# Low parts of weights for the second mixer, made in the first feed-forward, kept in DRAM and read back a pair of tiles ahead

## The chip, the cores and the metric

The kernel runs on one core of a Trainium2 chip (trn2). The metric is the device time of one execution in microseconds; the median of three executions of the kernel before is 2540.43 us (2537.12 to 2541.62). TensorE is PE in the profile, its weight load PEld, VectorE DVE, ScalarE ACT, GpSimd POOL and SyncE SP. All DMAs of the kernel before are issued by SP.

## The reference

Two blocks follow each other. The first has two layers over 256 tokens of a latent and 256 of a context, 1024 wide. A layer is a mixer and a feed-forward, each modulated from a condition vector (adaLN) and closed by a gated residual and a layer norm. In the second layer the context is needed only for keys, values and states, so that layer works on 256 columns where the first works on 512. The second block, two layers of another kind, follows and is not touched. What the change concerns is the mixer of the second layer of the first block:

```python
def _latent_mixer(h, mem, cos, sin, p):
    proj = h @ p['w_in']
    k, v, kg, vg, gf, gb = _mem_parts(proj[..., :MEM_COLS], p)
    q, qg, r, glu, gates = _rest_parts(proj[..., MEM_COLS:], p)
    ...
    o_att = _attend_blocks(_apply_rope(q, cos, sin), k_all, v_all)
    o_gla, _, _ = _gla_bidir(qg, kg, vg, gf, gb, s_f, s_b)
    return _merge(o_att, o_gla, r, glu, gates, p)

def _conv_module(glu, p):
    a, g = jnp.split(glu, 2, axis=-1)
    y = a * jax.nn.sigmoid(g)
    pad = CONV_WIDTH // 2
    y = lax.conv_general_dilated(y, p['conv_w_dw'].astype(y.dtype), (1,), [(pad, pad)], ...)
    y = jax.nn.silu(_layernorm(y, p['conv_ln_g'], p['conv_ln_b']))
    return y @ p['w_conv_o']

def _merge(o_att, o_gla, r, glu, gates, p):
    ...
    g_att, g_gla, g_conv = jnp.split(jax.nn.sigmoid(gates), N_BRANCH, axis=-1)
    return (g_att * y_att + g_gla * y_gla + g_conv * y_conv) @ p['w_out']
```

The conv is depthwise, 31 taps wide over 1024 channels, and its layer norm goes over the channels. All is in float32.

## The kernel before

A float32 product is made of three matmuls of reduced-width operands. Each weight tile is split into a high part `whi` (a cast by ACT) and a low part `wlo` (raw minus high, a subtraction by DVE, on some tiles by POOL); each activation is kept as `hi` and `lo`. `mm_fm` and `mm_tm` then add high x high, high x low and low x high into one PSUM tile (L386 to L388 and L467 to L469). Weights are loaded as 1 MB `raw` tiles by SP, two buffers (`rp`); `whi` and `wlo` have three buffers each (`hp`, `lp`). One `raw` of 256 columns by 1024 rows gives two tiles of 128 columns in `fm`; in `proj_tm` it holds four row tiles of 512 columns, split two at a time. `wsplit` makes the parts of both.

The program is traced by Python and ordered by a list scheduler: every engine runs its instructions in the order that it gives, and `pri` moves an instruction forward or back in priority. Work beside the projections is put into lanes (`bg`): a lane is a list of generators and a rate, and each tile of a projection calls `tick`, which advances every lane by its rate in steps. A lane is emptied by `flush`.

The mixer of a layer (`mixer`) projects the conv's columns a and g first, in four pairs of tiles; after each pair (`L1504`) a generator `conv` is put into the lane "conv" with the rate CRATE0 in the first layer and CRATE1 in the second. It does two channel tiles: one ACT instruction and then 30 taps for each tile, `ca<-gt,cw,ca` on DVE, two taps per tile in a step; at the end POOL adds the two tiles into `cs`. Then come the projections of k and v (512 columns), of q (2 x 512), the columns for the gated linear attention (GLA, with its decay logs, `gla_logs`, on ACT), and of the GLA's values. Merge 0 multiplies the attention's output by `w_att_o` and by its gate; the gate tiles are ACT's `mt`. After it the lanes "gla" and "conv" are emptied, and `conv_norm` begins: a matmul of `cs` with `ones_d` (L1347) gives the mean of all channels, and then come subtraction, squares, their sum, the scale, tanh and the split into `hi` and `lo`. Merge 2 is that of the conv: eight gate tiles are projected ahead (PRE2), beside `conv_norm` and the GLA's scores, and then the conv's output, which needs `conv_norm`'s end.

The first feed-forward is that of layer 0, over 512 columns. Beside it the lane "ada" makes the second layer's modulation. Both are emptied before the second closing norm of that layer.

Places in the profile: the first feed-forward runs from about 825 to 1225 us, the second mixer from 1225 to about 1720. In the latter a, g and k lie in 1226 to 1300, q in 1300 to 1350, GLA's logs in 1400 to 1475, merge 0 to about 1503, merge 2 from there.

```python
    self.bg("conv", [self.conv(l, (m, m + 1), glu, acc, csum, cw, len(xs))], (CRATE0, CRATE1)[l])
    ...
    merge(0, "w_att_o", oatt, PRE0[l], ("heads", "att"), None if GLE[l] else logs)
    self.flush("gla", "conv")
    self.bg("conv", [self.conv_norm(l, acc, csum, ocv, T)], (NRATE0, NRATE1)[l])
    merge(2, "w_conv_o", ocv, PRE2[l], ("conv",))
```

Of the kernel before, what the change touches and what calls it, by code (L numbers as in the profile page):

```python
# [9 lines left out]
F32 = mybir.dt.float32  # L10
# [15 lines left out]
CRATE1 = 1.0  # L26
# [4 lines left out]
CP = 600  # L31
PLO0A = 0
# [155 lines left out]
class Builder:  # L188
    NU = 71

    def __init__(self, ctx, tc, ins, out, dbg=None, stop=None):
# [20 lines left out]
        self.lp = P(name="lp", bufs=3)  # L212
        self.pm = P(name="pm", bufs=3, space=PSUM)
# [143 lines left out]
    def wsplit(self, src, shape, pri=None):  # L357
        hi = self.hp.tile(list(shape), F32R, tag="whi", name=self.nm("whi"))
        lo = self.lp.tile(list(shape), F32R, tag="wlo", name=self.nm("wlo"))
        self.nsplit += 1  # L360
        with self.pri(self.wpri if pri is None else pri):
            self.nc.scalar.copy(hi, src)  # L362
            on_pool = self.pool_lo and self.nsplit % self.pool_lo == 0
            after = self.lo_behind.pop() if self.lo_behind else None
            with self.tc.issue_after(after.ins) if after else nullcontext():
                self.tt(lo, src, hi.bitcast(F32), ALU.subtract, self.nc.gpsimd if on_pool else None)
        return hi, lo

    def fm(self, w, c0, ncols, nk=8):

        raw = None
        for m in range(ncols // 128):
            if m % 2 == 0:
                raw = self.load_raw(w, 0, nk, c0 + m * 128, min(256, ncols - m * 128))
            o = (m % 2) * 128
            yield self.wsplit(raw[:, :, o : o + 128], (128, nk, 128))

    def mm_fm(self, out, W, a, nk=8, first=True, last=True):
# [5 lines left out]
        for k in range(nk):  # L384
            mm = self.nc.tensor.matmul
            mm(out, lhsT=hi[:, k, :], rhs=a.hi[k], start=(first and k == 0), stop=False)  # L386
            mm(out, lhsT=hi[:, k, :], rhs=a.lo[k], start=False, stop=False)  # L387
            mm(out, lhsT=lo[:, k, :], rhs=a.hi[k], start=False, stop=(last and k == nk - 1))  # L388
# [82 lines left out]
    def proj_tm(self, specs, nk, a, tts, consumer, hold=0, mid=None, between=None, ks=None, late=None, held=None, need=None, hook=False):  # L471
# [8 lines left out]
        for part, kl in enumerate((ks[: nk - hold], ks[nk - hold :])):  # L480
# [8 lines left out]
            for h, (w, r0, c0, ncols) in enumerate(specs):  # L489
                for run in runs:  # L490
# [6 lines left out]
                    for k2 in range(0, n4, 2):  # L497
# [3 lines left out]
                        hi, lo = self.wsplit(raw[:, k2 : k2 + n2, :], (128, n2, ncols))  # L501
                        for t in tts:
                            for k in range(n2):
                                kk = run[k2 + k]
                                self.mm_tm(ps[t, h], a, t, kk, (hi[:, k, :], lo[:, k, :]), kk == ks[0], kk == ks[-1])
# [1254 lines left out]
    def layer1(self, l):  # L1760
# [33 lines left out]
        if l == 0:  # L1794
            self.bg("ada", [self.ada(1, (1, 0, 4, 3, 2, 5))], AD1)
        if T == 512:
# [10 lines left out]
            self.flush("ada")  # L1807
# [373 lines left out]
```

## Time and profile before

| what | value |
|---|---|
| median of three executions | 2540.43 us (2537.12 to 2541.62) |
| profiled execution, its own time | 2540.03 us |
| its span | 2538.2 us, mean granted clock 0.982 |
| PE, DVE, ACT, POOL busy | 2405.4, 1624.2, 1180.4, 521.2 us |
| DMA | 345.39 MB, mean 136 GB/s; HBM written 1.05 MB |
| DMA queues | SP's q1 41.5% of the 16 engines' span, instruction queues 0.4% |

The profile is one execution. The page gives busy time by engine; the table by windows gives the same for any stretch; the waits name, for each line of an engine, what it stood for; the timeline lists single instructions with the idle time before them in brackets and what ended it. A busy share over the whole span says little: stretches with different limits lie behind each other.

### The profile page before, as it was taken

How to read it: one execution, taken by the hardware profiler on the slowest of the kernel's cores; microseconds unless marked ns; L12 is line 12 of the kernel's file. 1: busy time of each engine (PE TensorE's matmuls, PEld its weight loads, DVE VectorE, ACT ScalarE, POOL GpSimd, SP SyncE). 2: the span in 40 equal slices, each digit the busy share in tenths (PEclk: the TensorE clock that was granted, in tenths of full speed). 3: DMA queues.
4: the chain of work that ended last, by engine and by line, in shares of the span. 5: the costliest groups of instructions: out<-in, count | busy, mean ns of one | idle time of the engine just before them, and what ended most of it. 6: DMA issues, size and time to landing. Idle time of an engine off the chain costs nothing. (4 is left out here: it accounts for less than half of the span.)

```text
span 2538.2 us, 38571 instructions
## 1 busy us (share of the span) xinstructions
PE 2405.4 (95%) x15163; PEld 2066.3 (81%) x15163; DVE 1624.2 (64%) x2700; ACT 1180.4 (47%) x2225; POOL 521.2 (21%) x460
## 2 busy tenths in 40 slices
PE   7989999899999999999889987998999999999998
PEld 4767887688877777778879887888987899887997
DVE  5878997984365433343899597676625656556564
ACT  3223577654343322232536945654443644446443
POOL 1002003790014000003310006531072100102001
PEclk9999999999999999999999998999999999999999
DMA  8432212223433545553342252643664246543454
GB/s 256 150 136 73 84 31 90 67 84 117 133 102 131 183 150 183 166 183 100 92 129 92 68 166 84 196 137 96 211 208 149 85 150 219 198 144 106 153 192 149
DMA packets 277689, 345.39 MB, mean 136 GB/s; under 512 B 12894, under 2 KB 208888, under 8 KB 277508
## 3 DMA queue, kind: packets, MB, share of 16 engines
q1 hardware_dynamic: 277508, 342.94, 41.5%
q8 instruction: 119, 1.95, 0.3%
q14 instruction: 62, 0.51, 0.1%
HBM read 341.85 MB, written 1.05 MB: 135 GB/s over the span
## 5 line engine op out<-in xcount | busy, mean ns | idle before, releaser
L386 PE MATMUL pm<-hi,whi 128*128 128x256 f32 (+1 forms) x2824 | 917.8, 327 | 24.5 <-ACT mt L298 13.1
L388 PE MATMUL pm<-hi,wlo 128*128 128x256 f32 (+1 forms) x2824 | 909.6, 323 | 6.8 <-DVE wlo L288 6.6
L387 PE MATMUL pm<-lo,whi 128*128 128x256 f32 (+1 forms) x2824 | 910.7, 323 | 4.1 <-POOL lo L288 2.7
L362 ACT CAST whi<-raw 128x1024 fp32r<-128x1024 f32 (+1 forms) x464 | 484.5, 1049 | 829.4 <-PE pm L387 518.9
L288 DVE TENSOR_TENSOR wlo<-raw,whi 128x1024 fp32r<-128x1024 f32 (+2 forms) x437 | 550.9, 1264 | 423.5 <-ACT whi L362 400.0
L386 PEld LDWEIGHTS pm<-hi,whi 128*128 128x128 f32 x2824 | 540.2, 192 | 69.8 <-ACT mt L298 13.9
L388 PEld LDWEIGHTS pm<-hi,wlo 128*128 128x128 f32 x2824 | 541.1, 192 | 52.4 <-DVE wlo L288 8.9
L387 PEld LDWEIGHTS pm<-lo,whi 128*128 128x128 f32 x2824 | 542.0, 192 | 48.3 <-issue 4.1
L291 DVE SCALAR_TENSOR_TENSOR ca<-gt,cw,ca 128x242 f32<-128x242 f32 (+28 forms) x480 | 267.4, 608 | 0.2
L467 PE MATMUL pm<-whi,hi 128*128 128x512 f32 x536 | 212.8, 397 | 7.9 <-DVE qn L288 3.6
L468 PE MATMUL pm<-wlo,hi 128*128 128x512 f32 x536 | 210.6, 393 | 8.9 <-DVE wlo L288 7.7
L469 PE MATMUL pm<-whi,lo 128*128 128x512 f32 x536 | 210.2, 392 | 0.0
L288 POOL TENSOR_TENSOR s<-s,mhalf 128x1 f32<-128x1 f32 (+2 forms) x82 | 66.9, 816 | 481.2 <-DVE s L295 474.1
L288 POOL TENSOR_TENSOR hl<-hr,hh 128x512 fp32r<-128x512 f32 (+1 forms) x38 | 56.0, 1477 | 467.4 <-ACT hh L454 328.1
L467 PEld LDWEIGHTS pm<-whi,hi 128*128 128x128 f32 x536 | 101.3, 189 | 31.3 <-issue 5.4
L468 PEld LDWEIGHTS pm<-wlo,hi 128*128 128x128 f32 x536 | 101.3, 189 | 30.0 <-DVE wlo L288 8.1
L469 PEld LDWEIGHTS pm<-whi,lo 128*128 128x128 f32 x536 | 101.2, 189 | 22.0 <-issue 0.8
L288 POOL TENSOR_TENSOR ek<-B 128x256 f32<-128x256 f32 (+1 forms) x100 | 102.0, 1039 | 1.1 <-DVE mt L288 0.6
L288 POOL TENSOR_TENSOR eq<-B 128x256 f32<-128x256 f32 x96 | 89.8, 955 | 49.0 <-DVE ptot L291 27.7
L288 POOL TENSOR_TENSOR wlo<-raw,whi 128x1024 fp32r<-128x1024 f32 (+1 forms) x35 | 81.1, 2330 | 84.3 <-ACT whi L362 78.0
L467 PE MATMUL pm<-hh,hi 128*128 128x512 f32 (+2 forms) x258 | 92.4, 361 | 4.8 <-ACT hi L768 2.3
L468 PE MATMUL pm<-hl,hi 128*128 128x512 f32 (+2 forms) x258 | 93.0, 361 | 1.3 <-POOL hl L288 0.9
(327 smaller groups left out, 3350.2 us busy)
## 6 DMA issues: line engine op xcount, KB each, us to landing
raw<-in_w_in_dram SPq DMA_DIRECT2D x84, 1024.0 KB
aw<-in_w_ada_dram SPq DMA_DIRECT2D x192, 256.0 KB
raw<-in_w_gate_up_dram SPq DMA_DIRECT2D x40, 1024.0 KB
raw<-in_w_ff_gate_dram SPq DMA_DIRECT2D x21, 1024.0 KB
raw<-in_w_ff_up_dram SPq DMA_DIRECT2D x21, 1024.0 KB
raw<-in_w_down_dram SPq DMA_DIRECT2D x20, 1024.0 KB
raw<-in_w_ff_down_dram SPq DMA_DIRECT2D x18, 1024.0 KB
raw<-in_w_att_o_dram SPq DMA_DIRECT2D x8, 1024.0 KB
```

The source lines that it names most:

```text
L288: return (eng or self.nc.vector).tensor_tensor(out=out, in0=a, in1=b, op=op)
L291: return self.nc.vector.scalar_tensor_tensor(out=out, in0=a, scalar=s, in1=b, op0=op0, op1=op1)
L362: self.nc.scalar.copy(hi, src)
L386: mm(out, lhsT=hi[:, k, :], rhs=a.hi[k], start=(first and k == 0), stop=False)
L387: mm(out, lhsT=hi[:, k, :], rhs=a.lo[k], start=False, stop=False)
L388: mm(out, lhsT=lo[:, k, :], rhs=a.hi[k], start=False, stop=(last and k == nk - 1))
L467: f(p, lhsT=a.hi[kk][:, sl], rhs=hi, start=first, stop=False)
L468: f(p, lhsT=a.hi[kk][:, sl], rhs=lo, start=False, stop=False)
L469: return f(p, lhsT=a.lo[kk][:, sl], rhs=hi, start=False, stop=last)
```

## The change

Two numbers are new or changed: CRATE1 goes from 1.0 to 1.2, and the lane "early" gets the rate 0.8. In the first feed-forward this lane (`lo_ahead`) works through part of the second layer's `w_in`: six blocks of 256 columns, those of a and g from the second pair of tiles on, and the 512 columns of k and v. It does so in 32 steps. In each, POOL's queue loads 256 KB (`er`), ACT casts it (`eh`), DVE subtracts (`el`), and POOL's queue writes the low part to DRAM tiles `dl`, in two writes of 128 KB for a and g, in one of 256 KB for k: 32 loads and 56 writes. The lane is emptied together with "ada".

In the second mixer `lo_back` reads the low parts into `wl` tiles on SP's queue, 32 reads of 256 KB; `fm` calls it one pair of tiles ahead, `proj_tm` at the tile. `wsplit` then casts the high part only, so that 16 subtractions of 128x1024 do not run there. Raw weights are loaded as before. `mm_fm` and `mm_tm` take the low part from two or more tiles.

```diff
--- before.py
+++ after.py
@@ -23,12 +23,14 @@
           "g": 5664, "gate": 6688}
 WP = -100
 CRATE0 = 1.3
-CRATE1 = 1.0
+CRATE1 = 1.2
 ARATE0 = 0.6
 ARATE1 = 0.6
 GRATE0 = 0.8
 GRATE1 = 0.6
 CP = 600
+ERATE = 0.8
+LBP = -200
 PLO0A = 0
 PLO0B = 0
 PLO0 = PLO0A, PLO0B
@@ -210,6 +212,8 @@
         self.rp = P(name="rp", bufs=2)
         self.hp = P(name="hp", bufs=3)
         self.lp = P(name="lp", bufs=3)
+        self.dp = P(name="dp", bufs=1, space=bass.MemoryType.DRAM)
+        self.early = {}
         self.pm = P(name="pm", bufs=3, space=PSUM)
         self.ps = P(name="ps", bufs=5, space=PSUM)
 
@@ -354,8 +358,54 @@
             self.nc.sync.dma_start(t, src)
         return t
 
-    def wsplit(self, src, shape, pri=None):
+    def lo_ahead(self, w, fms, tms):
+
+        nc = self.nc
+
+        def part(src, n, outs):
+            raw = self.u((128, n, 512 // n), F32, "er")
+            nc.gpsimd.dma_start(raw, src)
+            hi, lo = self.u((128, n, 512 // n), F32R, "eh"), self.u((128, n, 512 // n), F32R, "el")
+            nc.scalar.copy(hi, raw)
+            self.tt(lo, raw, hi.bitcast(F32), ALU.subtract)
+            for o, c in outs:
+                nc.gpsimd.dma_start(o, (lo[:, :, c] if n > 1 else lo[:, 0, c]).bitcast(F32))
+
+        for c0 in fms:
+            d = [[self.dp.tile([128, 4, 128], F32, name=self.nm("dl")) for _ in range(2)] for _ in range(2)]
+            for k in range(0, 8, 2):
+                part(w[k * 128 : k * 128 + 256, c0 : c0 + 256].rearrange("(k p) c -> p k c", p=128), 2,
+                     [(d[m][k // 4][:, k % 4 : k % 4 + 2, :], slice(128 * m, 128 * m + 128)) for m in range(2)])
+                if k == 6:
+                    for m in range(2):
+                        self.early[w.tensor.name, w.offset, 0, c0 + 128 * m] = d[m]
+                yield
+        for c0 in tms:
+            for k in range(8):
+                d = self.dp.tile([128, 512], F32, name=self.nm("dl"))
+                part(w[k * 128 : k * 128 + 128, c0 : c0 + 512].unsqueeze(1), 1, [(d, slice(0, 512))])
+                self.early[w.tensor.name, w.offset, k * 128, c0] = [d]
+                yield
+
+    def lo_back(self, w, r0, c0):
+
+        ds = self.early.pop((w.tensor.name, w.offset, r0, c0), None)
+        if ds is None:
+            return None
+        out = []
+        for d in ds:
+            t = self.u(d.shape, F32R, "wl")
+            with self.pri(LBP):
+                self.nc.sync.dma_start(t.bitcast(F32), d)
+            out.append(t)
+        return out
+
+    def wsplit(self, src, shape, pri=None, los=None):
         hi = self.hp.tile(list(shape), F32R, tag="whi", name=self.nm("whi"))
+        if los:
+            with self.pri(self.wpri if pri is None else pri):
+                self.nc.scalar.copy(hi, src)
+            return hi, los
         lo = self.lp.tile(list(shape), F32R, tag="wlo", name=self.nm("wlo"))
         self.nsplit += 1
         with self.pri(self.wpri if pri is None else pri):
@@ -369,11 +419,14 @@
     def fm(self, w, c0, ncols, nk=8):
 
         raw = None
+        back = lambda m: [self.lo_back(w, 0, c0 + (m + j) * 128) for j in range(2)]
+        nxt = back(0)
         for m in range(ncols // 128):
             if m % 2 == 0:
+                ls, nxt = nxt, back(m + 2)
                 raw = self.load_raw(w, 0, nk, c0 + m * 128, min(256, ncols - m * 128))
             o = (m % 2) * 128
-            yield self.wsplit(raw[:, :, o : o + 128], (128, nk, 128))
+            yield self.wsplit(raw[:, :, o : o + 128], (128, nk, 128), los=ls[m % 2])
 
     def mm_fm(self, out, W, a, nk=8, first=True, last=True):
         if isinstance(a, Pair):
@@ -383,9 +436,10 @@
         hi, lo = W
         for k in range(nk):
             mm = self.nc.tensor.matmul
+            lk = lo[k // 4][:, k % 4, :] if isinstance(lo, list) else lo[:, k, :]
             mm(out, lhsT=hi[:, k, :], rhs=a.hi[k], start=(first and k == 0), stop=False)
             mm(out, lhsT=hi[:, k, :], rhs=a.lo[k], start=False, stop=False)
-            mm(out, lhsT=lo[:, k, :], rhs=a.hi[k], start=False, stop=(last and k == nk - 1))
+            mm(out, lhsT=lk, rhs=a.hi[k], start=False, stop=(last and k == nk - 1))
 
     def proj_fm(self, w, c0, ncols, a, T, fm=None, done=()):
 
@@ -498,11 +552,13 @@
                         n2 = min(2, n4 - k2)
                         if need:
                             need(run[k2])
-                        hi, lo = self.wsplit(raw[:, k2 : k2 + n2, :], (128, n2, ncols))
+                        ls = [self.lo_back(w, r0 + run[k2 + k] * 128, c0) for k in range(n2)]
+                        ls = [x[0] for x in ls] if all(ls) else None
+                        hi, lo = self.wsplit(raw[:, k2 : k2 + n2, :], (128, n2, ncols), los=ls)
                         for t in tts:
                             for k in range(n2):
                                 kk = run[k2 + k]
-                                self.mm_tm(ps[t, h], a, t, kk, (hi[:, k, :], lo[:, k, :]), kk == ks[0], kk == ks[-1])
+                                self.mm_tm(ps[t, h], a, t, kk, (hi[:, k, :], lo[k] if ls else lo[:, k, :]), kk == ks[0], kk == ks[-1])
                             if run[k2 + n2 - 1] == ks[-1]:
                                 consumer(t, h, ps[t, h])
                         self.tick()
@@ -1793,6 +1849,8 @@
             return
         if l == 0:
             self.bg("ada", [self.ada(1, (1, 0, 4, 3, 2, 5))], AD1)
+            cols = [IN_OFF[n] + 256 * i for i in range(1, 4) for n in "ag"]
+            self.bg("early", [self.lo_ahead(I["w_in"][1], cols, [IN_OFF["k"]])], ERATE)
         if T == 512:
             g = self.ffn_up(wg, 0, wu, 0, 0, 12, a, T, mid)
             gates = self.gates(l, 5, xs)
@@ -1804,7 +1862,7 @@
                 self.proj_tm([(wd, 0, hf * 512, 512)], 12, g, range(4), c)
             pre = lambda: self.bg("pre", [self.prehold([(wd, 12 * 128, 512, 512)], PW3, 8, 2)])
             g = self.ffn_up(wg, 0, wu, 0, 12, 22, a, T, None, pre if PH2 else None)
-            self.flush("ada")
+            self.flush("ada", "early")
             self.a1 = Pair(self.act_alloc(8, 256), self.act_alloc(8, 256))
             part1 = lambda s: self.mod_T(1, s, 0, [nts.pop((s, t)) for t in range(2)], self.a1.parts[s], 0, False)
             last = (0, 0)
```

DVE, at the end of merge 0 and the start of merge 2 in the second mixer. `ca<-gt,cw,ca` are taps of the last pair of channel tiles, `mt<-mt,pm` closes a tile of merge 0, `ca<-ca,ps` is the first subtraction of the conv norm. Before (merge 0's eight `mt` stand at 1587 to 1625):

```order
1643 L291 SCALAR_TENSOR_TENSOR ca_10463<-gt_11090,cw_10624,ca_10463 128x242
1644 L288 TENSOR_TENSOR wlo_13912<-raw_13865,whi_13911 128x1024
1645 L291 SCALAR_TENSOR_TENSOR ca_10464<-gt_11126,cw_10624,ca_10464 128x242
1646 L291 SCALAR_TENSOR_TENSOR ca_10463<-gt_11090,cw_10624,ca_10463 128x241
1647 L291 SCALAR_TENSOR_TENSOR ca_10464<-gt_11126,cw_10624,ca_10464 128x241
1648 L288 TENSOR_TENSOR wlo_13973<-raw_13970,whi_13972 128x1024
1649 L288 TENSOR_TENSOR ca_10457<-ca_10457,ps_13658 128x256
1650 L288 TENSOR_TENSOR ca_10458<-ca_10458,ps_13658 128x256
1651 L288 TENSOR_TENSOR ca_10459<-ca_10459,ps_13658 128x256
```

Now:

```order
1639 L292 TENSOR_TENSOR wlo_13654<-raw_13611,whi_13653 128x1024
1640 L295 SCALAR_TENSOR_TENSOR ca_10746<-gt_11440,cw_10922,ca_10746 128x242
1641 L295 SCALAR_TENSOR_TENSOR ca_10745<-gt_11406,cw_10922,ca_10745 128x241
1642 L295 SCALAR_TENSOR_TENSOR ca_10746<-gt_11440,cw_10922,ca_10746 128x241
1643 L292 TENSOR_TENSOR wlo_13686<-raw_13683,whi_13685 128x1024
1644 L292 TENSOR_TENSOR wlo_13716<-raw_13683,whi_13715 128x1024
1645 L292 TENSOR_TENSOR wlo_13748<-raw_13745,whi_13747 128x1024
1646 L295 SCALAR_TENSOR_TENSOR mt_13358<-mt_13358,pm_13689 128x256
1647 L292 TENSOR_TENSOR wlo_13778<-raw_13745,whi_13777 128x1024
```

The last tap stood 22 rows behind the last `mt` of merge 0 and directly ahead of the conv norm's subtraction, and now stands four rows ahead of the first `mt`.

PE, at the start of merge 2, where `ones_d` is the mean over the channels and `pm` the gate tiles of merge 2. Before:

```order
7027 L387 MATMUL pm_13871<-lo_10011,whi_13867 128x256
7028 L388 MATMUL pm_13871<-hi_10007,wlo_13868 128x256
7029 L386 MATMUL pm_13871<-hi_10008,whi_13867 128x256
7030 L387 MATMUL pm_13871<-lo_10012,whi_13867 128x256
7031 L1347 MATMUL ps_13658<-cs_10465,ones_d 128x256
7032 L388 MATMUL pm_13871<-hi_10008,wlo_13868 128x256
7033 L386 MATMUL pm_13871<-hi_10008,whi_13867 128x256
7034 L387 MATMUL pm_13871<-lo_10012,whi_13867 128x256
```

Now:

```order
6948 L442 MATMUL pm_13946<-hi_10292,wlo_13943 128x256
6949 L440 MATMUL pm_13946<-hi_10292,whi_13942 128x256
6950 L441 MATMUL pm_13946<-lo_10296,whi_13942 128x256
6951 L442 MATMUL pm_13946<-hi_10292,wlo_13943 128x256
6952 L1403 MATMUL ps_13972<-cs_10747,ones_d 128x256
6953 L440 MATMUL pm_14000<-hi_10289,whi_13996 128x256
6954 L441 MATMUL pm_14000<-lo_10293,whi_13996 128x256
6955 L442 MATMUL pm_14000<-hi_10289,wlo_13997 128x256
```

The `ones_d` matmul stood behind four gate tiles and eight matmuls of a fifth, and now stands behind one gate tile.

SP, at the projections of g's last pair, k and v, and q. `raw<-in_w_in` of 128x8x256 is a pair of tiles of a or g, of 128x4x512 half of the rows of k and v or of q; `rope` and `gain` are tables for the norms of q and k. Before:

```order
377 L354 DMA raw_10988<-in_w_in_dram 128x8x256
378 L354 DMA raw_11059<-in_w_in_dram 128x8x256
379 L354 DMA raw_11160<-in_w_in_dram 128x4x512
380 L354 DMA raw_11229<-in_w_in_dram 128x4x512
381 L354 DMA raw_11363<-in_w_in_dram 128x4x512
382 L874 DMA rope_11137<-in_rope_dram 128x512
383 L877 DMA gain_11139<-in_q_norm_dram 128x128
384 L877 DMA gain_11146<-in_k_norm_dram 128x128
```

Now:

```order
398 L358 DMA raw_11377<-in_w_in_dram 128x8x256
399 L399 DMA wl_11227<-dl_8971 128x512
400 L399 DMA wl_11229<-dl_8972 128x512
401 L399 DMA wl_11231<-dl_8973 128x512
402 L399 DMA wl_11233<-dl_8974 128x512
403 L358 DMA raw_11477<-in_w_in_dram 128x4x512
404 L358 DMA raw_11551<-in_w_in_dram 128x4x512
405 L358 DMA raw_11689<-in_w_in_dram 128x4x512
406 L930 DMA rope_11454<-in_rope_dram 128x512
407 L933 DMA gain_11456<-in_q_norm_dram 128x128
408 L933 DMA gain_11463<-in_k_norm_dram 128x128
409 L399 DMA wl_11479<-dl_9203 128x512
```

The reads of the last g pair stand between its raw load and k's; those of k stand behind k's two raw loads, the first raw load of q and the three tables.

## Rows read from the trace of the kernel before

**Rows 1.** the page's busy line: busy us (share of span) and number of instructions
```profile
PE 2405.4 (95%) x15163; PEld 2066.3 (81%) x15163; DVE 1624.2 (64%) x2700; ACT 1180.4 (47%) x2225; POOL 521.2 (21%) x460
```

**Rows 2.** busy us per stretch: PE, PEld, DVE, ACT, POOL, granted clock, DMA share, GB/s
```profile
1226.00:1300.00 74.00, 66.30 (x442) 60.91 (x440) 65.10 (x125) 35.64 (x64) 12.87 (x11) 0.95 0.44 136
1300.00:1350.00 50.00, 42.19 (x244) 36.36 (x245) 43.63 (x90) 22.04 (x67) 8.26 (x8) 0.97 0.36 108
1400.00:1475.00 75.00, 72.06 (x436) 63.74 (x435) 43.88 (x90) 70.18 (x105) 1.54 (x2) 1.00 0.27 84
1475.00:1500.00 25.00, 25.00 (x211) 25.00 (x210) 24.05 (x46) 11.25 (x13) 0.00 (x0) 1.00 0.57 176
1500.00:1525.00 25.00, 18.15 (x136) 17.56 (x135) 19.64 (x41) 7.97 (x12) 3.79 (x4) 0.93 0.52 161
1525.00:1550.00 25.00, 14.55 (x86) 13.99 (x87) 21.10 (x32) 15.87 (x38) 18.47 (x22) 0.73 0.26 85
```

**Rows 3.** waits of PE in 1200 to 1560: us in total, times, longest
```profile
PE pm L386 <- ACT mt L298: 13.1, 4, 6.7
PE ps L1347 <- POOL cs L288: 5.3, 1, 5.3
PE ps L1311 <- DMA cwr<-in_conv_w_dw_dram: 3.4, 2, 2.0
...
PE pm L467 <- DVE qn L288: 2.2, 2, 1.7
```

**Rows 4.** timeline of PE, 1512 to 1520: start, us, shape, count
```profile
1513.86 0.28 PE L387 MATMUL pm<-lo,whi 128*128 128x256 f32 x1
1519.48 1.22 PE L1347 MATMUL ps<-cs,ones_d 128*128 128x256 f32 x2 [5.35 <-POOL cs L288]
```

**Rows 5.** timeline of DVE and of POOL, 1508 to 1521, same columns
```profile
1508.93 2.00 DVE L291 SCALAR_TENSOR_TENSOR ca<-gt,cw,ca 128x246 f32<-128x246 f32 x5
...
1516.83 1.22 DVE L288 TENSOR_TENSOR wlo<-raw,whi 128x1024 fp32r<-128x1024 f32 x1
1520.74 1.08 DVE L288 TENSOR_TENSOR ca<-ca,ps 128x256 f32<-128x256 f32 x3 [2.69 <-PE ps L1347]
...
1516.71 2.72 POOL L288 TENSOR_TENSOR cs<-cs,ca 128x256 f32<-128x256 f32 x2 [106.63 <-DVE ca L291]
```

**Rows 6.** the low parts on DVE in 1226 to 1300: busy us, mean ns, idle before
```profile
L288 DVE TENSOR_TENSOR wlo<-raw,whi 128x1024 fp32r<-128x1024 f32 x19 | 23.2, 1232 | 5.1 <-ACT whi L362 5.1
```

**Rows 7.** busy time of DVE in the taps alone, by stretch: us (count), clock, DMA share
```profile
1300.00:1345.00 45.00, 11.99 (x26) 0.96 0.39 120
...
1400.00:1471.00 71.00, 6.82 (x17) 1.00 0.24 74
1471.00:1517.00 46.00, 25.21 (x60) 1.00 0.59 184
```

**Rows 8.** DMA in 1226 to 1300: packets, bytes, mean rate
```profile
DMA packets 7818, 10.03 MB, mean 136 GB/s; under 512 B 194, under 2 KB 5570, under 8 KB 7813
```

**Rows 9.** timeline of SP and DVE: when DMAs are issued, when a gain lands
```profile
1279.59 0.38 SPq L877 DMA_DIRECT2D gain<-in_q_norm_dram  x1
...
1285.99 0.23 DVE L295 TENSOR_SCALAR gain<-gain 128x128 f32<-128x128 f32 x1 [1.02 <-DMA gain<-in_q_norm_dram]
```

**Rows 10.** one burst of twelve 256 KB loads, and the rate while it lands
```profile
1617.57 9.51 SPq L447 DMA_DIRECT2D hr<-in_w_out_dram  x12
...
1617.00:1637.00 20.00, 19.50 (x212) 18.57 (x211) 10.80 (x17) 11.31 (x24) 1.02 (x1) 1.00 0.95 317
```

**Rows 11.** 850 to 1200, the first feed-forward: one window, groups of ACT and DVE
```profile
850.00:1200.00 350.00, 350.00 (x1640) 272.73 (x1640) 134.46 (x161) 97.62 (x127) 35.69 (x21) 1.00 0.49 166
...
L454 ACT CAST hh<-hr 128x512 fp32r<-128x512 f32 x8 | 4.9, 610 | 0.0
...
L288 DVE TENSOR_TENSOR fg<-fg,pm 128x512 f32<-128x512 f32 x20 | 13.7, 687 | 45.3 <-PE pm L388 45.3
```

## The prediction

> **What bounds the kernel now.** I read the page first, then a table of stretches through the second mixer, then the waits of PE there, then the timeline at the longest of them. PE is busy 95% of the span [rows 1], so only stretches in which PE stands still can pay. The first feed-forward is not one: in 850 to 1200 PE is busy 350.00 of 350.00 us, DVE 134.46, ACT 97.62 and POOL 35.69 [rows 11]. There the other engines have room and PE has none. The second mixer is where PE stands [rows 2]: 7.7 us idle in 1226 to 1300, 7.8 in 1300 to 1350, 6.9 in 1500 to 1525 and 10.5 in 1525 to 1550, the last two at a granted clock of 0.93 and 0.73. In the first two stretches DVE is the engine that is full (65.10 of 74 and 43.63 of 50). In 1400 to 1475 it is ACT (70.18 of 75) and DVE has 31 us free. The waits name the ends [rows 3]: 13.1 us for ACT's `mt`, of which the timeline puts 6.8 and 5.5 behind the conv norm, and 5.3 us in one piece for POOL's `cs`.
>
> That one piece can be followed back. PE stops after its matmul of 1513.86 and starts the `ones_d` matmul, the mean over the conv channels, at 1519.48 [rows 4]. It needs `cs`, which POOL adds in 2.72 us from 1516.71, having stood 106.63 us for DVE's `ca` [rows 5]; and `ca` are the last two tiles of the 31-tap convolution, 60 taps that DVE works through in 1471 to 1517, 25.21 us of taps [rows 7] between low parts. So the last conv taps on DVE set when the mean can be taken. Behind the mean stands a chain (subtract, square, variance, scale, tanh, split) in which DVE's first subtraction starts at 1520.74 [rows 5]; PE has gate tiles of merge 2 to run beside it, eight of them, and runs out.
>
> **The change part by part.**
>
> *Low parts leave DVE in the second mixer.* Sixteen `wlo` go (twelve of the columns a and g, four of k and v), at 1.232 us [rows 6] 19.7 us of DVE in a stretch where DVE is full.
>
> *The taps that take their place.* The conv lane's rate goes from 1.0 to 1.2. By the order, 120 taps stand between the conv weights and the first `vl`, where 74 stood; 14 of the 16 low parts left that piece. In: 46 x 0.42 us (25.21 over 60, [rows 7]) = 19.3; out: 14 x 1.232 = 17.2. DVE's work up to the k norm is the same within 2 us. So I do not give the a, g and k stretch DVE's relief as a gain; what it gets is the earlier cast-to-matmul path (no low part between), set against the loads below.
>
> *The q projection.* In 1300 to 1345 stand 26 taps, 11.99 us [rows 7], between the norms that PE waits for (`qn`, 2.2 us in two [rows 3]); the order has none left there. Of PE's 7.8 idle us in 1300 to 1350 I give back 4; the ends are 0 (another engine is next, POOL's `s`) and 6.
>
> *The last taps and the mean.* This is the main term. In the order DVE's last tap stands before merge 0's first `mt`, and before it stood after the last. On PE the `ones_d` matmul then stands 24 rows behind merge 0, one gate tile, where it stood 4 tiles and 8 matmuls behind it: 80 matmuls of 128x256 earlier. In 1475 to 1500 211 matmuls take 25.00 us [rows 2], 0.1185 each, so 80 x 0.1185 = 9.5 us earlier in PE's own work. The wait of 5.35 us goes as well, since the last tap is done several tiles ahead; together 14.8 us by which the norm chain starts ahead of where PE then stands. What PE can get back is its idle time there: 6.9 + 10.5 = 17.3 us [rows 2], and the slow clock: 14.55 us of PE at 0.73 and 18.15 at 0.93 are 3.9 + 1.3 = 5.2 us more than at full clock. I take 14.8 plus about 1 of the clock, **16**. Ends: 20 (all the idle time and half of the clock's), and 8 (the 5.35 and a quarter of the rest, where the chain behind the mean becomes longer because POOL's scores and DVE's low parts of merge 2 now stand in it).
>
> *Taps in the ACT-bound stretch.* Where do the 60 taps of 1471 to 1517 go? Into 1400 to 1475, where 17 stand now (6.82 us, [rows 7]) and DVE has 31 us free [rows 2]; 25 us fit. They stand in blocks of up to 13 ahead of a low part, 5.5 us. PE has two tiles of whi and wlo in hand there, 2 x 24 matmuls at 72.06/436 = 0.165 us, 7.9 us. A block alone is covered; a block after a late cast is not. I take +2, ends 0 and +5.
>
> *The read-back.* 32 loads of 256 KB on SP's queue, 8.4 MB, into a stretch that moves 10.03 MB in 74 us [rows 8]: 18.4 MB, 249 GB/s. The nearest row is a burst of the same shape on the same queue: twelve loads issued in 9.51 us while DMA runs at 317 GB/s [rows 10]. At that rate 18.4 MB take 58 of 74 us, so it fits when spread. Per 256 columns it is 2.1 MB, 6.6 us, against 48 x 0.1185 = 5.7 us of PE: paced by DMA, 0.9 x 6 pairs = 5.6 us, where nothing else is slower; but PE needs more than 5.7 now, since it idles there. The low parts of k and v stand on SP behind the first load of q, which waits for k's own buffer. Issued there, the `gain` of 64 KB took 1279.59 to 1285.99, 6.4 us, to be usable behind a 1 MB load [rows 9]; a tile of PE, 24 x 0.1185 = 2.8 us, covers part. Against this, the load of the conv weights, `cwr` (3.4 us of PE's wait, [rows 3]), no longer stands behind the fifth load of a and g. I take **-2** for the stretch, ends -7 and +4.
>
> *Making them in the first feed-forward.* 32 steps, each a 256 KB load and one or two writes on POOL's queue (88 in all), a cast on ACT (0.610 us by the nearest row) and a subtraction on DVE (0.687) [rows 11]: 19.5 us of ACT and 22.0 of DVE beside 350 us in which both are more than half idle. DMA goes from 166 to about 166 + 16.8 MB/400 us = 208 GB/s, of 317 seen [rows 10, 11]. No row shows a DMA issued by POOL. From below, SP issues one in 0.38 us [rows 9]; from above, POOL is full only if 88 issues take the 360 us that it has free in 400, 4.1 us each. Nothing on POOL there is close to PE. I take +1, ends 0 and +6.
>
> The Trainium skill, "DMA: Bandwidth & Descriptors", section "Anatomy of one DMA — SWDGE (gpsimd) path", has a price for it: a fixed 2.0 us and the bytes at 436 GB/s. My estimate from that page is 2.6 us for 256 KB and 2.3 for 128 KB, some 211 us for all 88 if POOL stood through each; the sum by it stays as it is, since that is under the 360.
>
> Sum: -16 - 4 + 2 - 2 + 1 = **-19 us**. The profiled execution took 2540.03 us (span 2538.2) and the median of three is 2540.43, so both bases are the same: 2521 us.
>
> **The rivals.**
>
> *A. The read-back eats its stretch* (0.17). k's low parts come 6.4 us after their place, and DMA's pace costs 3 of its 5.6: the a, g and k stretch is +6, not -2, and the conv gain is kept at 14. For it: SP's order and the `gain` row [rows 9]. Against: the DMA share is 0.44 there [rows 2]. -14 - 4 + 2 + 6 + 1 = -9: 2531.
>
> *B. The gain is handed back* (0.13). The mean comes earlier, but what comes behind it, ACT's squares and tanh, POOL's scores (POOL is busy 18.47 of 25 us in 1525 to 1550, [rows 2]), ends when it did. Then -5 remains of the conv term, +5 in the logs' stretch, and the front at 0: 2540.
>
> *C. The feed-forward stands still* (0.13). ACT and DVE take their work in order, so a cast that waits for its load on POOL's queue holds back the casts of PE's tiles, and the subtraction holds PSUM's evacuation. PE's cover is two tiles, 48 x 350/1640 = 10.2 us [rows 11]. The 6.4 us of the `gain` behind one load [rows 9] is within it; behind two loads, with POOL's own wait, it can be 11. The change turns to a loss where a step costs more than 19/32 = 0.6 us beyond the cover. At 11 us it is 0.8 x 32 = 26 us, net +7: 2547, and more where two steps fall into one cover. Against: 32 steps lie among some 78 tiles of 5.1 us.
> The Trainium skill, "DMA: Bandwidth & Descriptors", section "Issuing engines are not separate DMA queues", speaks for this case: loads that POOL starts interleave with SP's on the same 16 engines. No run here shows it yet; by it the `er` come later and the raws too.
>
> *D. It doesn't do what it says*: the rate of 1.2 moves the taps and the low parts are beside the point. Then the same taps with the low parts still on DVE would do; but DVE is 65.10 of 74 full [rows 2] and 19.3 us of taps do not fit. It is a question of cause, with no time of its own and no chance beside the forecast's.
>
> **How the numbers follow.** Forecast 0.57 at 2521, its own range 2508 to 2531; A 0.17; B 0.13; C 0.13. About 0.2%, 5 us, is what a measurement of this kernel can tell from no change. Faster by more: all of the forecast, A but 0.02: 0.72. Same: B's most and A's edge, 0.14. Slower: C and a little of B, 0.14. The range reaches from the sum of the good ends (-20 - 6 - 7 = -33, 2507) to 2541, which takes in A and half of B and leaves out C.
>
> **What would show it.** Right: the `ones_d` matmul has no wait for `cs` and PE's idle time in what was 1500 to 1550 falls from 17 us to a few; no `qn` wait in the q projection; PE at 25 of 25 in the first feed-forward; `wl` loads ending before the matmuls that read them. Wrong: a wait of PE for a `wl` of k over 5 us (A); the wait for `mt` as long as before, only elsewhere (B); PE short of 350 in the first feed-forward, with ACT waiting for `er` (C).

## The result and the profile after

The changed kernel takes 2555.65 us (median of four, 2552.77 to 2559.41) where the kernel before took 2538.77 beside it; the ratio is 1.0064, 95% interval 1.0047 to 1.0081. It is slower by 16 to 17 us. The profiled execution took 2559.41 us, its span is 2557.7.

Both traces hold 15163 matmuls, so the start of the n-th matmul can be set against the n-th of before. The table gives how far the later kernel is behind at some places, and in brackets what the stretch up to there added. (The profiles wander by up to 2.5 us ahead of the first feed-forward, where the kernels are still the same.)

| up to | before, us | changed | added |
|---|---|---|---|
| first feed-forward, just begun | 819.0 | +0.6 | |
| its middle | 1068.6 | +25.2 | (+24.6) |
| its end, second mixer's start | 1226.7 | +27.0 | (+1.8) |
| within a and g | 1252.8 | +22.1 | (-4.8) |
| end of a and g | 1272.6 | +24.3 | (+2.2) |
| k done, q | 1306.5 | +33.0 | (+8.7) |
| GLA's columns | 1358.5 | +31.5 | (-1.5) |
| merge 2's start | 1509.9 | +33.2 | (+1.8) |
| conv's output | 1552.6 | +17.3 | (-16.0) |
| GLA's scores | 1604.9 | +19.5 | (+2.2) |
| end | 2527.5 | +19.7 | (+0.2) |

So the conv norm brought what was forecast, and two stretches ahead of it (the first feed-forward, 26.4, and that of k, 8.7) lost twice that. The windows of the changed kernel say the same (busy us of PE, PEld, DVE, ACT, POOL; granted clock; DMA share; GB/s); [rows 2, 11] answer to them, though from 1226 on the same work lies 17 to 33 us later here:

```profile
850.00:1200.00 350.00, 331.82 (x1529) 255.80 (x1528) 145.07 (x178) 110.47 (x155) 87.26 (x103) 0.98 0.61 203
1226.00:1300.00 74.00, 67.38 (x474) 63.34 (x473) 56.81 (x122) 40.16 (x71) 22.20 (x25) 0.95 0.57 183
1300.00:1350.00 50.00, 39.55 (x170) 31.20 (x170) 41.14 (x100) 15.83 (x43) 6.00 (x7) 0.93 0.41 134
1500.00:1525.00 25.00, 24.18 (x202) 23.98 (x201) 18.58 (x28) 11.73 (x16) 4.77 (x4) 1.00 0.56 181
1525.00:1550.00 25.00, 23.18 (x186) 22.64 (x186) 17.14 (x26) 11.66 (x20) 6.93 (x8) 0.98 0.53 159
```

PE, which had 350.00 of 350 in the first feed-forward, has 331.82, at a clock of 0.98. No engine there is near full: ACT 110.47 of 350, DVE 145.07, POOL 87.26, DMA 0.61. It is a matter of who waits for whom. PE's waits in 850 to 1165 (us in total, times, longest):

```profile
PE pm L521 <- DVE z L292: 8.3, 1, 8.3
PE ps L692 <- DMA aw<-in_w_ada_dram: 5.5, 4, 3.8
PE pm L440 <- DVE fg L295: 4.4, 2, 2.3
```

A few long stalls, not one at each of the 32 steps. The longest can be followed back through four timelines of the changed kernel (start, us, engine, operation; in brackets the idle time ahead and what ended it), first PE, then DVE, ACT and POOL:

```profile
1025.06 0.39 PE L523 MATMUL ps<-whi,lo 128*128 128x512 f32 x1
1033.73 0.79 PE L521 MATMUL pm<-whi,hi 128*128 128x512 f32 x1 [8.29 <-DVE z L292]
...
1032.39 0.69 DVE L292 TENSOR_TENSOR el<-er,eh 128x512 fp32r<-128x512 f32 x1 [5.80 <-ACT eh L369]
1033.00 1.88 DVE L292 TENSOR_TENSOR z<-pm,gb 128x512 f32<-128x512 f32 x3
...
1024.52 1.34 ACT L369 CAST eh<-er 128x512 fp32r<-128x512 f32 x2 [3.17 <-DMA er<-in_w_in_dram]
1031.74 0.62 ACT L369 CAST eh<-er 128x512 fp32r<-128x512 f32 x1 [5.87 <-DMA dl<-el]
...
1026.17 1.45 POOL L372 DMA_DIRECT2D dl<-el  x2 [6.33 <-DVE el L292]
1027.62 0.73 POOL L367 DMA_DIRECT2D er<-in_w_in_dram  x1
```

PE needs a PSUM bank. DVE would free it with `z` at 1033.00 but works in order and stands 5.80 us in front of a subtraction `el`, which stands for ACT's cast `eh` at 1031.74, which stands 5.87 us for its load; and that load was issued by POOL only at 1027.62, behind two writes that had to wait 6.33 us for the subtraction of a step before. So a step's load stands in a queue behind the writes of a step before it. (The wait of ACT is put down to a DMA `dl`; the load issued at 1027.62 is the one that the cast reads.) With that one ACT waits 41.2 us in nine times for `er` over the stretch:

```profile
ACT eh L369 <- DMA er<-in_w_in_dram: 35.3, 8, 8.2
ACT eh L369 <- DMA dl<-el: 5.9, 1, 5.9
```

POOL's own share is a wait too: 212.1 us ahead of `dl`, for DVE's `el`. Not all of PE's waits go back to a cast: the 5.5 us for `aw`, a weight of the modulation that SP loads, have another end, which these rows don't follow back.

The stop costs more than its own length, since the granted clock is lower after it: after PE stood 8.29 us it is 0.51 for 3.3 us, the level of 1.2 GHz, and then 1.00, that of 2.4. The rows are these two windows, and then the whole feed-forward, the same 1953 matmuls, before and now:

```profile
1033.70:1037.00 3.30, 3.27 (x8) 2.59 (x9) 1.77 (x3) 0.00 (x0) 3.28 (x4) 0.51 0.92 310
1037.00:1040.00 3.00, 3.00 (x15) 2.48 (x14) 0.00 (x0) 0.00 (x0) 2.98 (x4) 1.00 0.37 103
...
819.00:1226.70 407.70, 401.30 (x1953) 318.58 (x1952) 177.88 (x241) 122.20 (x169) 55.00 (x45) 0.99 0.45 150
...
819.60:1253.70 434.10, 410.71 (x1953) 324.85 (x1952) 198.90 (x273) 139.13 (x200) 112.97 (x130) 0.97 0.55 185
```

Of the 26.4 us, 17.0 are more idle time of PE, and 9.4 are the same matmuls run at a lower clock.

The second place is k. PE's waits in 1235 to 1345, and the timelines of PE and SP there:

```profile
PE pm L522 <- DMA wl<-dl: 5.2, 1, 5.2
PE pm L440 <- ACT ga L1548: 3.5, 3, 2.3
PE pm L521 <- DVE qn L292: 3.4, 2, 2.6
PE ps L1367 <- DMA cwr<-in_conv_w_dw_dram: 1.6, 1, 1.6
```

```profile
1308.69 0.80 PE L522 MATMUL pm<-wl,hi 128*128 128x512 f32 x1 [5.19 <-DMA wl<-dl]
...
1286.93 13.25 SPq L358 DMA_DIRECT2D raw<-in_w_in_dram  x3
1300.23 0.50 SPq L930 DMA_DIRECT2D rope<-in_rope_dram  x1
1301.94 6.50 SPq L399 DMA_DIRECT2D wl<-dl  x8
```

SP issues the eight reads of k's low parts from 1301.94 on, behind three raw loads which, with its waits between them, take it 13.25 us, and PE reaches the first of them at 1303.5. The wait for `cwr` has halved (3.4 in [rows 3]), and nothing waits for `cs`: POOL adds it at 1508.08, and PE takes the mean when it comes there:

```profile
1508.08 2.72 POOL L292 TENSOR_TENSOR cs<-cs,ca 128x256 f32<-128x256 f32 x2 [88.90 <-DVE ca L295]
```

### The profile page after: what moved, and what is told of

It reads as the page before. It is cut to its first block, busy times and chain, and to the rows that moved or that the text cites. A ratio compares the mean times of both kernels' runs of the same rounds, so it can differ in the third digit from the quotient of the medians.

```text
span 2557.7 us, 38908 instructions
## 1 busy us (share of the span) xinstructions
PE 2415.4 (94%) x15163; PEld 2070.9 (81%) x15163; DVE 1629.9 (64%) x2716; ACT 1197.3 (47%) x2257; POOL 577.5 (23%) x548
## 5 line engine op out<-in xcount | busy, mean ns | idle before, releaser
L442 PE MATMUL pm<-hi,wlo 128*128 128x256 f32 (+1 forms) x2728 | 885.4, 325 | 5.7 <-DVE wlo L292 5.6
L412 ACT CAST whi<-raw 128x1024 fp32r<-128x1024 f32 (+1 forms) x448 | 467.8, 1048 | 756.7 <-PE pm L441 526.2
L292 DVE TENSOR_TENSOR wlo<-raw,whi 128x1024 fp32r<-128x1024 f32 (+2 forms) x421 | 532.7, 1269 | 385.3 <-ACT whi L412 379.6
L442 PEld LDWEIGHTS pm<-hi,wlo 128*128 128x128 f32 x2728 | 525.6, 193 | 47.2 <-DVE wlo L292 7.6
L295 DVE SCALAR_TENSOR_TENSOR ca<-gt,cw,ca 128x244 f32<-128x244 f32 (+29 forms) x480 | 264.0, 609 | 0.9 <-ACT ca L302 0.7
L522 PE MATMUL pm<-wlo,hi 128*128 128x512 f32 x512 | 202.1, 395 | 8.9 <-DVE wlo L292 7.7
L292 POOL TENSOR_TENSOR ek<-B 128x256 f32<-128x256 f32 (+1 forms) x100 | 93.8, 957 | 2.4 <-PE ps L1263 1.8
```

The lines of the kernel that those rows point to most:

```text
L292: return (eng or self.nc.vector).tensor_tensor(out=out, in0=a, in1=b, op=op)
L295: return self.nc.vector.scalar_tensor_tensor(out=out, in0=a, scalar=s, in1=b, op0=op0, op1=op1)
L442: mm(out, lhsT=lk, rhs=a.hi[k], start=False, stop=(last and k == nk - 1))
L522: f(p, lhsT=a.hi[kk][:, sl], rhs=lo, start=False, stop=False)
```

## The experiments

All are timed against the kernel before on the same chip. "By stretch" means the table's method: the n-th matmul against before's.

**The tap rate alone.** The kernel before with one number changed.

```diff
-CRATE1 = 1.0
+CRATE1 = 1.2
```

> The kernel before with CRATE1 at 1.2 and nothing else. By the order DVE's last conv tap stands ahead of merge 0's first tile here too. If the tap rate alone moves the conv norm, merge 2's stretch gains the 16 us that the changed kernel shows there, and the a, g, k and q stretch loses 19 us of taps less the 9 us that DVE is idle in it, +10: about 2533 us in all. If the low parts' leaving DVE is what makes the gain, the stretch ahead loses all 16 again or more: 2538 to 2550 us.

Measured: 2529.22 us, ratio 0.9953 (0.9936 to 0.9970). By stretch: first feed-forward 0, a to q +1.1, up to merge 2 +2.9, conv norm **-17.3**, then +2.2. The conv gain is the rate's, whole, and the stretch ahead pays 1 us, not 10. The taps' rows (DVE busy in taps, count, clock, DMA share) show why; [rows 7] are before's:

```profile
1226.00:1300.00 74.00, 33.49 (x76) 0.93 0.44 135
1300.00:1345.00 45.00, 11.66 (x26) 0.92 0.40 120
1345.00:1400.00 55.00, 27.95 (x65) 1.00 0.26 81
1400.00:1471.00 71.00, 26.33 (x65) 1.00 0.25 75
1471.00:1517.00 46.00, 6.59 (x17) 0.97 0.60 184
```

The rate puts one tap more ahead of k's norm (75 by the order, 74 before): it fills the stretch in which ACT is the bound, 65 taps in 1400 to 1471 where 17 stood, and leaves 17 where 60 stood. DVE had 31 us free there.

**Making without reading back.** The rate is 1.0 and `lo_back` finds nothing, so the second mixer subtracts as before; the making stays.

```diff
-CRATE1 = 1.2
+CRATE1 = 1.0
-        ds = self.early.pop((w.tensor.name, w.offset, r0, c0), None)
+        ds = None
```

> The low parts are made and written in the first feed-forward, but nothing reads them back, the second mixer subtracts as before, CRATE1 is 1.0 (all that is left out is the read-back; DRAM tiles stay unused). If the feed-forward's loss belongs to the making, it is +26 us there and nothing after it: 2565 us. If part of it came with the second mixer's new order, less.

Measured: 2563.03 us, ratio 1.0088 (1.0067 to 1.0109). By stretch: first feed-forward +25.5, all the rest +2. The same three waits of PE stand in the feed-forward as in the changed kernel:

```profile
PE pm L521 <- DVE z L292: 8.7, 1, 8.7
PE ps L692 <- DMA aw<-in_w_ada_dram: 4.5, 3, 3.8
PE pm L440 <- DVE fg L295: 4.4, 2, 2.3
```

The loss belongs to the making alone.

**Loads two steps ahead, and one.** The steps of `lo_ahead` are put in a list, and each step first issues the load of a later one.

```diff
+        raws = [load(i) for i in range(AHEAD)]
+        for i, (src, n, outs, keys) in enumerate(steps):
+            if i + AHEAD < len(steps):
+                raws.append(load(i + AHEAD))
+            raw = raws.pop(0)
...
             nc.scalar.copy(hi, raw)
```

> The changed kernel with the loads of the low parts' raw weights issued two steps ahead, ahead of the writes that wait for the subtraction. If PE stands in the first feed-forward because ACT, in order, waits for a load that POOL issued late, the 26 us fall to 8 or less: 2537 us or less. If the cause is the DMA engines' being shared, or the casts and subtractions themselves, they stay above 18: 2548 us or more.

> The changed kernel with the loads in the first feed-forward issued one step ahead instead of two. In the changed kernel a load stands 3 to 16 us ahead of its cast (median about 7) and lands in 4.4 us (median), with two steps about 20 us ahead. If the stall is a matter of that lead alone, one step gives about 12 us and takes most of the 25 us away: 0 to 6 us left in the feed-forward, 2533 to 2540 us. If what helped in the run with two steps was another order of POOL's writes, 10 us or more are left.

Measured with two steps: 2533.94 us, ratio 0.9972 (0.9961 to 0.9983); the first feed-forward adds 0.2 us. With one: 2535.15 us, ratio 0.9986 (0.9974 to 0.9997); it adds 5.4. Behind it both are by stretch within 2 us of the changed kernel. From a load's issue to its cast there are 7.3 us in the changed kernel (median of 32), 15.5 with one step, 19.9 with two. The rows are 850 to 1200 with two steps and ACT's waits for `er` in 850 to 1165, then, with one step, the same wait and PE's only one in 850 to 1165:

```profile
850.00:1200.00 350.00, 349.87 (x1639) 272.57 (x1638) 158.93 (x198) 113.54 (x159) 94.27 (x106) 1.00 0.63 211
...
ACT eh L390 <- DMA er<-in_w_in_dram: 0.2, 1, 0.2
```

```profile
ACT eh L390 <- DMA er<-in_w_in_dram: 8.9, 4, 4.2
...
PE ps L699 <- DMA aw<-in_w_ada_dram: 4.0, 3, 2.9
```

The same 88 DMAs, casts and subtractions run with two steps, at a DMA share of 0.63 against 0.61, and PE has 349.87 of 350. So neither the sharing of the DMA engines nor the added work has to cost the 25 us; the place of the loads in POOL's queue decides. With one step ACT still waits 8.9 us for `er`, but no evacuation holds PE: what is left there is `aw`. One thing is not held still: with loads ahead the list scheduler also puts casts up to three weight tiles earlier into ACT's order (counted by the `whi` ahead of each). No run moves the loads and keeps the casts where they stood.

**The DMAs alone.** Casts and subtractions of the making are left out; the raw values are written in place of the low parts.

```diff
-            nc.scalar.copy(hi, raw)
-            self.tt(lo, raw, hi.bitcast(F32), ALU.subtract)
             for o, c in outs:
-                nc.gpsimd.dma_start(o, (lo[:, :, c] if n > 1 else lo[:, 0, c]).bitcast(F32))
+                nc.gpsimd.dma_start(o, raw[:, :, c] if n > 1 else raw[:, 0, c])
```

> The changed kernel without the 32 casts and 32 subtractions of the first feed-forward: the raw values are written to DRAM in place of the low parts (this part of the computation is left out), the DMAs on POOL's queue stay, all 88. If the wait of ACT and DVE in their order is the cause, the feed-forward's 26 us fall to 5 or less: 2535 us. If sharing the DMA engines is the cause (late loads of raw or aw), 15 or more stay: 2545 us or more.

Measured: 2534.63 us, ratio 0.9978 (0.9969 to 0.9988); the first feed-forward adds 4.2 us, two waits for a weight of the modulation:

```profile
PE ps L689 <- DMA aw<-in_w_ada_dram: 4.2, 2, 3.6
```

This is the part that sharing can have; the run with two steps shows that it need not be there either.

The Trainium skill, "DMA: Bandwidth & Descriptors", section "Issuing engines are not separate DMA queues", says that DMAs of several issuing engines interleave on the same 16 engines. The runs agree to this extent: with the DMAs alone the `aw` loads, of SP's queue, come late by up to 3.6 us. It is not what cost the 25 us.

**The read-back without the rate.** Loads two steps ahead, CRATE1 1.0.

```diff
-CRATE1 = 1.2
+CRATE1 = 1.0
```

> The changed kernel with loads two steps ahead (no stall in the first feed-forward) and CRATE1 back at 1.0. By the order the last conv tap stands behind merge 0 again. If the rate alone makes the conv gain, merge 2's stretch keeps its idle time (0 to -2 us there instead of -16) and what the read-back does in a, g, k and q is left alone: +5 us as with the rate at 1.2, 2545 us, or less if fewer taps ahead of k's norm help it. If the low parts' leaving DVE makes the conv gain, the time stays near 2534 us.

Measured: 2539.88 us, ratio 1.0002 (0.9993 to 1.0011). By stretch: a and g -4.4 and +0.5, k and q +6.0 and -1.8, conv norm -0.7. PE's waits in 1400 to 1560 are those of before [rows 3], though 16 subtractions have left DVE:

```profile
PE pm L447 <- ACT mt L303: 12.7, 4, 6.6
PE ps L1410 <- POOL cs L293: 4.2, 1, 4.2
```

So the read-back by itself, with k's reads late, is worth nothing here: what a and g gain, k and q give back.

**k's part of the read-back.** Three kernels with loads two steps ahead and the rate 1.2: only a and g made ahead; k's reads called at the third pair of a and g; and at the second pair.

```diff
-            self.bg("early", [self.lo_ahead(I["w_in"][1], cols, [IN_OFF["k"]])], ERATE)
+            self.bg("early", [self.lo_ahead(I["w_in"][1], cols, [])], ERATE)
```

```diff
+            if m == 4 and not start:
+                self.kback = {kk: self.lo_back(w, kk * 128, IN_OFF["k"]) for kk in range(8)}
...
-                        ls = [self.lo_back(w, r0 + run[k2 + k] * 128, c0) for k in range(n2)]
+                        ls = [self.kback.pop(run[k2 + k], None) if nk == 8 and c0 == IN_OFF["k"] else None for k in range(n2)]
```

(The third has `m == 2` there.)

> Loads two steps ahead, rate 1.2, and only the low parts of a and g made ahead; those of k and v are subtracted on DVE as before (four subtractions of 1.23 us back on DVE). If the 8.8 us lost between k and q come from k's read-back standing late on SP's queue (5.1 us of PE's wait), they fall to 0 to 3 and a and g keep their -4.7: 2525 to 2528 us. If they come from the taps that stand ahead of k's norm on DVE, they stay at 7 or more: 2533 us or above.

> Loads two steps ahead, rate 1.2, and the read-back of k's low parts called at the third pair of a and g, so that by the order all eight stand ahead of k's first raw load on SP. PE's wait for a low part of k (5.1 us) goes. If it was the cause of the 8.8 us: 2526 us. If the raw loads behind the eight reads now come late by 8 x 0.8 us, or DVE's taps hold k's norm: 2531 us or more.

> As the run before, with the read-back of k's low parts called one pair of tiles earlier, so that four of the eight stand ahead of the last raw load of g. The a and g stretch, paced by DMA, gives up 0 to 3 us of its 4.7; k's raw loads come 3 us earlier than in the run before. If DMA pace is what is left there, this is 1 to 3 us faster than that run; if DVE's taps ahead of k's norm are, it is the same within 1.

Measured: 2524.68 us, ratio 0.9934 (0.9918 to 0.9951); 2523.84 us, 0.9942 (0.9929 to 0.9955); 2524.72 us, 0.9941 (0.9928 to 0.9954). The three cannot be told apart. By stretch, beside the run with two steps and k's reads late:

| up to | k late | a and g only | third pair | second pair |
|---|---|---|---|---|
| within a and g | -4.7 | -4.4 | -4.9 | -4.6 |
| end of a and g | +2.2 | +0.5 | +2.2 | +5.2 |
| k done, q | +8.8 | -2.5 | +1.1 | -2.4 |
| GLA's columns | -1.5 | -0.1 | -1.3 | 0.0 |

PE waits for no `wl` in any of the three. With the reads at the third pair the table's other stretches are within 0.2 us of those with k late, and k and q cost 7.7 us less. That is the price of standing late in SP's queue: 5.1 us of PE's idle time and 2.6 of a lower clock behind it. The rows are the same stretch (end of a and g to "k done, q"), with k late and at the third pair:

```profile
1267.72:1310.40 42.68, 33.39 (x153) 27.03 (x152) 32.87 (x83) 12.15 (x28) 4.64 (x5) 0.92 0.44 148
...
1272.10:1307.10 35.00, 30.82 (x152) 25.53 (x151) 28.92 (x74) 11.78 (x24) 1.73 (x2) 1.00 0.49 164
```

What is left against the kernel without k's low parts (+1.1 against -2.5) goes with the taps, though no run moves them alone: PE's wait for the norm is 4.0 us there and 2.3 here, after 106 taps and 95 in 1226 to 1300. PE's waits in 1225 to 1350, with the reads at the third pair and then with a and g only:

```profile
PE pm L529 <- DVE qn L294: 4.0, 3, 2.2
```

```profile
PE pm L528 <- DVE qn L293: 2.3, 3, 1.5
```

At the second pair a and g cost 3 us more, and k gives them back. PE's wait there is for ACT's `ga`, which ACT takes behind three casts `whi` and eight instructions for `hf` and `hi`. That the reads slow a and g through DMA is not shown. PE's waits in 1225 to 1350:

```profile
PE pm L448 <- ACT ga L1556: 6.2, 3, 5.0
```

All three beat both kernels, by 31 us the changed one and by 15 the one before. Beside the rate alone, timed on another chip, they are 4 to 5 us lower by the medians and 3 to 5 by the ratios, whose intervals overlap (0.9918 to 0.9955 against 0.9936 to 0.9970). So it is not shown that the low parts, made and read back, are worth anything on top of the one number.

**Other rates.** The kernel before with CRATE1 at 1.1 and at 1.4.

```diff
-CRATE1 = 1.0
+CRATE1 = 1.1
```

> The kernel before with CRATE1 at 1.1 and nothing else. By the order the matmul of the conv's mean stands one gate tile behind merge 0, as with 1.2. If its place is what makes the gain, it is as with 1.2: 2529 us, within 3. If the gain goes with the number of taps done early, it is about half: 2534 us.

> The kernel before with CRATE1 at 1.4 and nothing else. The mean's matmul stands where it stands with 1.2. The taps are done earlier still. If only the place counts, it is 2529 us again, less or more what the taps cost in the stretch ahead of k's norm, where DVE has about 9 us free: 2529 to 2539 us.

Measured: 2531.58 us, ratio 0.9966 (0.9955 to 0.9978), and 2532.22 us, 0.9968 (0.9959 to 0.9978). The conv norm's stretch gains 14.1 and 14.7 us, the next one gives 4.9 and 5.0 back. By its time the run with 1.1 lies between its two forecasts, but 1.4, with more taps done early (8 left in 1471 to 1517, where 1.1 leaves 33), gains no more than 1.1. With all three rates the mean's matmul stands 80 matmuls earlier in PE's order than with 1.0. So its place goes with the gain and the number of early taps does not, and the intervals do not tell 1.1, 1.2 and 1.4 apart.

## Why the prediction was wrong

**The making: the step that failed.** The term was +1 with ends 0 and +6; it measured +25 (0.6 to 25.2 by the middle of the feed-forward, +26.4 to its end). The bound compared each engine's free time with the added work, and that was right and beside the point: with loads two steps ahead the same work costs 0.2 us. What was missed is order on one queue. The prediction took POOL as full or not full; it did not read from the order, in which loads and writes take turns, that a load stands behind writes which wait for DVE, and so a load's lead over its cast is a step's own chain, 7.3 us in the median, from 3.2 up, against a landing of 4.4 us in the median with SP's bursts ahead of it.

**Rival C had the mechanism, but the cover that it was held against, and with it the price, were wrong in kind.** It named the cast that waits for its load and the evacuation of PSUM behind the subtraction, and gave 26 us at 11 us a wait. But it was held against a cover of two weight tiles, 10.2 us, which is the cover of `whi` and `wlo`. `z` and `fg` have none like it: PE wants the bank that they free as soon as it gets there. So of nine waits of ACT, 41.2 us with a longest of 8.2, none was over the cover, and yet PE stood 12.7 us for `z` and `fg` in 850 to 1165. With the 5.5 for `aw` it makes 18.2 (315 less 296.82). Over the whole feed-forward PE's idle time grows by 17.0, and the lower clock costs 9.4. That 0.8 x 32 gave nearly the measured sum is chance.

```profile
850.00:1165.00 315.00, 296.82 (x1374) 226.82 (x1373) 130.50 (x164) 97.37 (x137) 70.88 (x95) 0.97 0.65 216
```

**The conv norm: size right, cause wrong.** The mean's matmul starts at 1537.4 where it started at 1519.48, in a program that is 33.2 us late at merge 2's start: 15.3 us earlier, against 14.8; the gain is 16.0, as forecast. But the prediction gave it to the low parts that leave DVE and set rival D aside without a chance, because 19.3 us of taps would not fit where DVE is full. They never had to: the rate alone puts 75 taps ahead of k's norm, not 120, and the rest where DVE was free, in a window whose 31 free us the prediction itself had named. The taps more ahead of k's norm are what fills DVE when the low parts have gone: with the read-back at a rate of 1.0 there are 104 by the order, 30 more than before, and with both 120. The rate alone gives 17.3, the read-back without the rate 0.7.

**The a, g and k stretch and q.** -2 and -4 were forecast, +4.5 came (27.0 to 31.5). a and g are better than the term (-4.8, then +2.2, where PE stands 2.3 us for ACT's `ga`); k lost 8.7, which is rival A: its 6.4 us for k's low parts came as a wait of 5.2, and its +6 for the stretch was near. The -4 in q came as -1.5. The prediction read PE's waits for `qn` as 2.2 us in two, but a third of 2.2 stands under another line, so they were 4.4 before. They are 4.1 now: the 26 taps are gone from between the norms, but the first wait is longer, 2.6, which fits the taps that moved ahead of k's norm. Nor is that piece of DVE's order "the same within 2 us": between the conv weights and the first `vl` stood 13 low parts and 2 are left, so 11 went there and not 14 (the other five stood ahead of it), 13.6 us against 19.3 of taps. The rows are of 1225 to 1350 before, and of 1225 to 1355 now:

```profile
PE pm L386 <- DVE qn L288: 2.2, 1, 2.2
...
PE pm L521 <- DVE qn L292: 4.1, 3, 2.6
```

**The logs' stretch** was +2 and is +1.8. Behind the conv +2.4 came that had no term.

**How the numbers were put together.** A and C were treated as other cases than the forecast. They are terms of the same sum: all three happened. With A's +6 for the stretch and C's 26 for the making, -16 - 4 + 2 + 6 + 26 = +14, 2554 us, and 2555.65 was measured. That it comes so near has luck in it, since C's 26 had. The range left C out, as it said.

The Trainium skill, "DMA: Bandwidth & Descriptors", section "Anatomy of one DMA — SWDGE (gpsimd) path", gave 2.6 and 2.3 us as estimates for a load and a write (all 88 come to 214 us by them and not to 211, which changes nothing). The trace has 0.73 us of POOL for issuing one, and medians of 4.4 and 3.7 us from issue to landing among SP's transfers; the page gives its fit per DMA and says nothing of other traffic beside it. The measurements decide, and it was the landing that mattered.

## What to carry to other kernels

When background work is threaded through a stage in which one engine is full, free time on the others says little: look at what stands behind each of its waits on every in-order engine, above all evacuations of PSUM, and issue its loads early enough on a queue where they don't stand behind writes that need the previous result. When a change sets two things at once, run each alone, the one-number one first; here that number brought 10 us, and what the rest adds to it, once its loads came early, was not clear of the intervals. And rivals that can happen beside the forecast are terms to be added, not cases to be chosen between.

## What the runs showed of the hardware

A DMA issue takes POOL about twice what it takes SP: 0.73 us against 0.38 [rows 9]. Loads of 256 KB on POOL's queue land in a median of 4.4 us here, and in 6.0 us with two steps ahead, where they cost nothing; the rows are of the DMA view (issues in 840 to 1165, KB each, median us to landing), first of the changed kernel, then of the one with two steps:

```profile
er<-in_w_in_dram POOLq DMA_DIRECT2D x30, 256.0 KB, 4.4
dl<-el POOLq DMA_DIRECT2D x48, 128.0 KB, 3.7
```

```profile
er<-in_w_in_dram POOLq DMA_DIRECT2D x28, 256.0 KB, 6.0
dl<-el POOLq DMA_DIRECT2D x48, 128.0 KB, 5.2
```

Beside a stage that moves 166 GB/s, another 45 GB/s of loads from DRAM and writes to it on a second queue can cost next to nothing: 211 GB/s at a PE of 349.87 of 350 us with two steps ahead. In the other kernels with two steps ahead PE's waits there are 0.6 to 1.2 us, all for `aw`.
